# S5 set-up in a fused mixer layer: its parameters are transposed eight places of the weight stream behind their fetch instead of one

## The chip, the cores and the metric

The kernel runs on one core of one Trainium2 chip. The metric is the device time of one execution in microseconds (us). The time before is the median of three runs, 1197.18 us (1196.2 to 1198.06). TensorE (PE) multiplies matrices, VectorE (DVE) does elementwise work and reductions, ScalarE (ACT) copies and activation functions, GpSimd (POOL) masks and some fetches, and SP issues most transfers.

## The reference

One decoder layer (D_MODEL 2048, 256 tokens, DEPTH 1) with three parallel token mixers:

```python
h = rms_norm(x, norm_w[i])
proj = h @ w_in[i]
(g_qkv, g_z, g_b, g_a, r_feat, r_z, s_u, s_z, gate_logits) = _split_cols(proj, SPLIT_SIZES)
o_a = gdn_branch(...)      # gated DeltaNet
o_b = rwkv7_branch(...)    # RWKV-7
o_c = s5_branch(s_u, s_z, s5_a_re[i], s5_a_im[i], s5_log_dt[i], ...)
branch_proj = jnp.einsum('blnc,ncd->blnd', branches, w_branch[i])
gates = jax.nn.sigmoid(gate_logits.reshape(bsz, seq, N_BRANCH, D_MODEL) + gate_b[i])
merged = jnp.sum(gates * branch_proj, axis=2)
x = x + (merged @ w_out[i])
return rms_norm(x, final_norm_w)
```

The S5 branch is a diagonal state-space model with 64 groups of 16 channels and 64 states a group. Its set-up turns three parameters, `a_re` and `a_im` (64 x 64 each) and `log_dt` (64), into the discrete coefficients that the scan needs:

```python
dt = jnp.exp(log_dt)[:, None]
mag = jnp.exp(a_re * dt)
ab_re, ab_im = mag * jnp.cos(a_im * dt), mag * jnp.sin(a_im * dt)
den = a_re * a_re + a_im * a_im
coef_re = ((ab_re - 1.0) * a_re + ab_im * a_im) / den
coef_im = (ab_im * a_re - (ab_re - 1.0) * a_im) / den
```

The products of the coefficients with `b` and `c`, a scan over the 256 tokens, a skip, a GELU and a GLU (`s5_glu_w`) follow.

## The kernel before

**The stream of weights.** Nearly all matmul work is one long stream of weight blocks. A block ("unit") is a tile of 128 x 1024 float32 values (512 KB). It is fetched on SP's queue (`load_unit`, L264) into one of four `raw` tiles, and split into a high and a low part, `whi` by ScalarE (L267) and `wlo` by VectorE (L268), three tiles each. Each of its eight k-steps is then multiplied three times: high by high, high by low, low by high (`mm_unit`, the matmuls recorded as L62). `run_stream` keeps two blocks loaded ahead in the order of the program.

**Mixer work between the blocks.** The small work of the three mixers is written as Python generators in named lanes. `pump` (L1103) is called behind the second, fourth and sixth of a block's eight k-steps and behind the block: four places a block, with two k-steps (six matmuls) from one place to the next. At each place each lane's `due` count falls by one, and while it is not above zero, the lane's generator is run to its next `yield`, whose number is added to the count. So the numbers in the yields space the steps of a lane in places. TensorE's instructions stay in the order of the program: every matmul and transpose goes through the object `pe`, which ties each to the one before. The other queues, SP's and VectorE's among them, are ordered by the framework's scheduler.

**The stretch of the change.** By about 612 us the input projections of all three mixers are done, the last of them S5's own input u (`got_su`, which stores u to memory as `uD`, L1092). The memory of the first stages (`fr`, with the tile pool `fp`) is released, and new tiles take its place. The lane `s` with `s5_all` is put up, and `run_stream(back1())` begins: for each of 16 column blocks, two gate projections (two units each; the first six of these gates are done earlier) and two branch projections (one unit each). `got_proj` takes the results into `merged`: L1250 for the first branch, L1252 and L1253 for the second. The first six units of this stream are therefore branch projections, the matmuls named `mm<-oT`. Behind `back1` come twelve units for S5's z path (`sz_job`). These two streams together have 384 places. Then `finish("s", "sm")` runs off whatever is left in S5's lanes, the results of S5 are split into `ysp`, and the second half of the stream begins: two z columns, the GLU's weights (which need `ysp`), the third branch and the output projection.

**The steps that the prediction follows.** `s5_setup` issues three small fetches on SP's queue (L1310, L1311, L1313: `a_re` and `a_im` into `s5raw`, `log_dt` into `s5ldt`). Then it yields. Its next step copies `log_dt`, spread over 64 columns, into the third part of `s5raw` on VectorE (L1315), transposes the three parts on TensorE (`s5t`), and copies them back as `s5par` (L1320). From there a long chain of small VectorE steps with a few on ScalarE works out the coefficients, spaced by further yields. When it ends, `s5_mats` (lane `sm`) and `s5_tile` (lane `s`) run over eight tiles of channels. For each tile, `s5_mats` fetches u back (`UX`, L1442) and `b` and `c`, builds `BX` on VectorE (L1457 to L1462) and transposes it on TensorE (`s5bt`). `s5_tile` ends with `s5y` on TensorE and the tile's part of the result `us` (L1602).

Of the kernel before, what the change touches and what calls it, by code (L numbers as in the profile page):

```python
# [36 lines left out]
def tile_trunk(  # L37
# [1270 lines left out]
    def s5_setup(sp):  # L1308
# [2 lines left out]
        nc.sync.dma_start(out=raw[:, 1], in_=s5_a_im[0].rearrange("(i g) n -> i (g n)", g=2))  # L1311
        ldt = sp.tile([32, 2], F32, name="s5ldt")
        nc.sync.dma_start(out=ldt, in_=s5_log_dt[0].rearrange("(i g) -> i g", g=2))  # L1313
        yield 1
        ve.tensor_copy(raw[:, 2].rearrange("p (g n) -> p g n", g=2), ldt.unsqueeze(2).to_broadcast([32, 2, 64]))  # L1315
        pt = br_bank("s5t")
        for j in range(3):
# [289 lines left out]
    def s5_all():  # L1607
        with tc.tile_pool(name="s5s", bufs=1, side="right") as sp:
            yield from s5_setup(sp)
        for t in range(8):  # L1610
            lane("sm", s5_mats(t))
        for t in range(8):
            yield from s5_tile(t)
# [146 lines left out]
```

## Time and profile before

| What | Value |
|---|---|
| median of three runs | 1197.18 us (1196.2 to 1198.06) |
| the profiled execution, whole | 1195.4 us |
| its span, first to last instruction | 1193.6 us |
| TensorE busy | 1168.8 us (98%) |
| VectorE busy | 905.6 us (76%) |
| ScalarE busy | 681.6 us (57%) |
| mean granted TensorE clock | 0.995 of full |
| moved by transfers | 203.97 MB, mean 171 GB/s |

The table is of one execution. Rows of the timeline give the start in us from the span's begin, the duration, the engine, the line of the kernel, the operation, the tile written and the tiles read; "x3" is a number of instructions merged into one row, and a bracket gives the idle time of the engine before it and what ended it. Line 62 and line 65 are helpers, through which all matmuls and all transposes go; there the tile names tell which step it is. Rows of the waits say who waited for whom, in us in total, the number of times, and the longest. The name of the one waited for is inferred from semaphore events, and a wait for several is put down to one of them. The ends of matmuls are modelled, so the distance from start to start tells more than a duration.

### The profile page before, as it was taken

How to read it: one execution, taken by the hardware profiler on the slowest of the kernel's cores; microseconds unless marked ns; L12 is line 12 of the kernel's file. 1: busy time of each engine (PE TensorE's matmuls, PEld its weight loads, DVE VectorE, ACT ScalarE, POOL GpSimd, SP SyncE). 2: the span in 40 equal slices, each digit the busy share in tenths (PEclk: the TensorE clock that was granted, in tenths of full speed). 3: DMA queues.
4: the chain of work that ended last, by engine and by line, in shares of the span. 5: the costliest groups of instructions: out<-in, count | busy, mean ns of one | idle time of the engine just before them, and what ended most of it. 6: DMA issues, size and time to landing. Idle time of an engine off the chain costs nothing. (4 is left out here: it accounts for less than half of the span.)

```text
span 1193.6 us, 29078 instructions
## 1 busy us (share of the span) xinstructions
PE 1168.8 (98%) x11534; PEld 1128.4 (95%) x11534; DVE 905.6 (76%) x2261; ACT 681.6 (57%) x1412; POOL 56.2 (5%) x92
## 2 busy tenths in 40 slices
PE   7999999999999999999989999999999999999997
PEld 7999999999999999999989999999999999999887
DVE  7879696879787888885569979999986665555555
ACT  5465767676767776766534555555544544444443
POOL 1000000000000000000020111111000000000000
PEclk9999999999999999999989999999999999999999
DMA  7766555555656555555657677777776666667763
GB/s 203 195 180 171 153 139 148 141 149 147 159 130 158 148 141 131 132 149 144 182 157 191 181 189 188 195 190 191 185 185 169 182 189 179 188 183 239 242 197 116
DMA packets 384642, 203.97 MB, mean 171 GB/s; under 512 B 38825, under 2 KB 376186, under 8 KB 384122
## 3 DMA queue, kind: packets, MB, share of 16 engines
q1 hardware_dynamic: 382650, 199.61, 62.1%
q0 software_dynamic: 1536, 1.58, 0.6%
q8 instruction: 91, 1.49, 0.5%
q10 hardware_dynamic: 320, 0.93, 0.2%
q14 instruction: 45, 0.37, 0.1%
HBM read 195.88 MB, written 6.18 MB: 169 GB/s over the span
## 5 line engine op out<-in xcount | busy, mean ns | idle before, releaser
L62 PE MATMUL mm<-hT,whi 128*128 128x256 f32 (+1 forms) x4160 | 782.1, 288 | 0.0
L62 PEld LDWEIGHTS mm<-hT,whi 128*128 128x128 f32 (+1 forms) x4160 | 644.6, 191 | 7.3 <-issue 1.2
L62 PE MATMUL mm<-hT,wlo 128*128 128x256 f32 (+1 forms) x2080 | 587.4, 282 | 0.0
L268 DVE TENSOR_TENSOR wlo<-raw,whi 128x1024 fp32r<-128x1024 f32 (+1 forms) x346 | 422.3, 1221 | 184.7 <-ACT whi L267 181.6
L267 ACT ACTIVATE whi<-raw 128x1024 fp32r<-128x1024 f32 (+1 forms) x346 | 365.2, 1056 | 320.2 <-PE mm L62 239.3
L62 PEld LDWEIGHTS mm<-hT,wlo 128*128 128x128 f32 (+1 forms) x2080 | 396.4, 191 | 0.0
L62 PE MATMUL mm<-oT,whi 128*128 128x256 f32 x768 | 142.8, 286 | 0.0
L62 PEld LDWEIGHTS mm<-oT,whi 128*128 128x128 f32 x768 | 120.9, 194 | 0.5 <-issue 0.4
L62 PE MATMUL mm<-oT,wlo 128*128 128x256 f32 x384 | 109.3, 285 | 0.0
L62 PE MATMUL mm<-whi,mT 128*128 128x512 f32 (+1 forms) x288 | 76.8, 354 | 0.0
L62 PEld LDWEIGHTS mm<-oT,wlo 128*128 128x128 f32 x384 | 74.2, 193 | 0.0
L62 PEld LDWEIGHTS mm<-whi,mT 128*128 128x128 f32 x288 | 51.2, 189 | 7.5
L62 PE MATMUL mm<-wlo,mT 128*128 128x512 f32 (+1 forms) x144 | 50.9, 354 | 0.0
L570 DVE TENSOR_TENSOR ivp<-ivZ,ivX 48x1 f32<-48x1 f32 (+14 forms) x120 | 34.6, 288 | 2.0
L688 DVE SCALAR_TENSOR_TENSOR scr<-mm,pv,scr 128x255 f32<-128x255 f32 (+2 forms) x72 | 34.1, 473 | 0.6
L62 PEld LDWEIGHTS mm<-wlo,mT 128*128 128x128 f32 x144 | 27.2, 189 | 3.8
L572 DVE TENSOR_REDUCE ivZ<-ivp 48x1 f32<-48x1 f32 (+14 forms) x120 | 27.3, 227 | 1.7
L62 PE MATMUL mm<-ysp,whi 128*128 128x256 f32 x128 | 23.1, 283 | 0.0
L1252 DVE SCALAR_TENSOR_TENSOR gate<-gate,mm 128x256 f32<-128x256 f32 x32 | 13.3, 417 | 12.1 <-PE mm L62 11.9
L1242 ACT ACTIVATE gate<-mm,hgate 128x256 f32<-128x256 f32 x48 | 22.1, 461 | 0.3
L691 ACT ACTIVATE gth<-scr 128x256 f32<-128x256 f32 x24 | 9.9, 414 | 21.4 <-DVE scr L688 17.8
L62 PEld LDWEIGHTS mm<-ysp,whi 128*128 128x128 f32 x128 | 19.8, 189 | 0.0
(541 smaller groups left out, 1278.4 us busy)
## 6 DMA issues: line engine op xcount, KB each, us to landing
raw<-in_w_in_dram SPq DMA_DIRECT2D x256, 512.0 KB
raw<-in_w_branch_dram SPq DMA_DIRECT2D x48, 512.0 KB
raw<-in_w_out_dram SPq DMA_DIRECT2D x32, 512.0 KB
raw<-in_s_glu_w_dram SPq DMA_DIRECT2D x8, 512.0 KB
xs<-in_x_dram SPq DMA_DIRECT2D x4, 512.0 KB
xr<-in_x_dram SPq DMA_DIRECT2D x2, 1024.0 KB
raw<-in_w_in_dram SPq DMA_DIRECT2D x4, 384.0 KB
gr<-grow SPq DMA_DIRECT2D x8, 128.0 KB
```

Of the source, the lines that this page charges most:

```text
L62: return self.put(nc.tensor.matmul(*a, **k).ins)
L267: u["top"] = lambda: se.activation(out=hi[:, 0:nn], in_=raw[:, 0:nn], func=AF.Copy)
L268: u["sub"] = lambda eng=ve: eng.tensor_tensor(out=lo[:, 0:nn], in0=raw[:, 0:nn], in1=hi[:, 0:nn].bitcast(F32), op=ALU.subtract)
L570: ve.tensor_tensor(out=pi, in0=Z[:, 0:i, 0:i].rearrange("p j c -> p c j"), in1=X[:, i, 0:i].unsqueeze(1).to_broadcast([8 * NU, i, i]), op= ...
L572: ve.tensor_reduce(out=Z[:, i, 0:i], in_=pi, axis=AX.X, op=ALU.add)
L688: ve.scalar_tensor_tensor(out=c[:, s:T], in0=p[:, 0:T - s], scalar=pv("cw", (3 - s) * 24 + col), in1=c[:, s:T], op0=ALU.mult, op1=ALU.add)
L691: se.activation(out=th, in_=c, func=AF.Tanh, scale=0.5)
L1242: se.activation(out=t, in_=pss[0][:, 0:T], func=AF.Tanh, scale=0.5, bias=hgate[:, b * 16 + i:b * 16 + i + 1])
L1252: ve.scalar_tensor_tensor(out=g, in0=g, scalar=1.0, in1=p0, op0=ALU.add, op1=ALU.mult)
```

## The change

One number: the first `yield` in `s5_setup`, between the issue of the three fetches and their first use, is 8 in place of 1. The numbers of all later yields stay as they are.

```diff
         nc.sync.dma_start(out=raw[:, 1], in_=s5_a_im[0].rearrange("(i g) n -> i (g n)", g=2))
         ldt = sp.tile([32, 2], F32, name="s5ldt")
         nc.sync.dma_start(out=ldt, in_=s5_log_dt[0].rearrange("(i g) -> i g", g=2))
-        yield 1
+        yield 8
         ve.tensor_copy(raw[:, 2].rearrange("p (g n) -> p g n", g=2), ldt.unsqueeze(2).to_broadcast([32, 2, 64]))
         pt = br_bank("s5t")
         for j in range(3):
```

## The prediction

> **What bounds the kernel now.** I read the page first, then who TensorE (PE) waits for, then the timelines of PE, of the transfer queue SP and of VectorE (DVE) around the place where PE waits.
>
> ```profile
> span 1193.6 us, 29078 instructions
> PE 1168.8 (98%) x11534; PEld 1128.4 (95%) x11534; DVE 905.6 (76%) x2261; ACT 681.6 (57%) x1412; POOL 56.2 (5%) x92
> ```
>
> PE is busy for 98% of the span. So a saving counts only where PE stands still or runs slowly. The list of what PE waited for, longest first, says where (us in total, times, longest):
>
> ```profile
> PE warm L65 <- DMA xs<-in_x_dram: 4.4, 1, 4.4
> PE s5t L65 <- DMA uD<-us: 4.0, 1, 4.0
> ```
>
> The first row is the start of the kernel. The second is the three transposes of S5's parameters, the step that the change moves. Asked from 600 us to the end, the same view gives this one row alone: after the s5t wait PE never waits again, so time saved there has a free way to the end. PE's timeline there (start, duration, engine, line, operation, count, idle before):
>
> ```profile
> 612.34 0.40 PE L62 MATMUL mm<-oT,whi 128*128 128x256 f32 x2
> ...
> 612.94 0.28 PE L62 MATMUL mm<-oT,wlo 128*128 128x256 f32 x1
> 617.21 0.69 PE L65 MATMUL s5t<-ident,s5raw 32*128 32x32 f32 x3 [3.99 <-DMA uD<-us]
> 617.82 0.80 PE L62 MATMUL mm<-oT,whi 128*128 128x256 f32 x2
> ...
> 622.47 0.55 PE L62 MATMUL mm<-oT,whi 128*128 128x256 f32 x2
> 622.85 0.28 PE L62 MATMUL mm<-oT,wlo 128*128 128x256 f32 x1
> 622.98 0.40 PE L62 MATMUL mm<-oT,whi 128*128 128x256 f32 x2
> ```
>
> Five matmuls lie between the starts 612.34 and 612.94, so one takes 0.12. After six of them PE could have gone on at 613.06; it stands until 617.21. Then eight groups of three (617.82 to 622.98, the first and the last shown) take 5.16 us where 24 x 0.12 = 2.88 would do. The stretches of time say why (stretch, length, busy time and count of PE, PEld, DVE, ACT, POOL; granted clock; DMA):
>
> ```profile
> 615.00:616.00 1.00, 0.00 (x0) 0.00 (x0) 0.85 (x1) 0.00 (x0) 1.00 (x2) 0.98 0.34 80
> 616.00:617.00 1.00, 0.00 (x0) 0.00 (x0) 0.00 (x0) 0.00 (x0) 1.00 (x2) 0.50 0.11 21
> ...
> 617.20:623.00 5.80, 5.79 (x28) 5.61 (x29) 3.57 (x19) 1.06 (x1) 4.49 (x10) 0.52 0.60 144
> 623.00:667.70 44.70, 44.70 (x374) 44.55 (x373) 43.00 (x172) 20.55 (x24) 0.25 (x1) 1.00 0.66 177
> ```
>
> The clock is granted in full until close to 616, falls to 0.50 some 2.8 us after PE stopped, is still 0.52 in the mean from 617.2 to 623, and is whole after that. The pause is paid twice, once in standing and once in slow matmuls.
>
> What PE waited for is named as a transfer; SP's queue and DVE show which:
>
> ```profile
> 613.68 0.34 SPq L1092 DMA_DIRECT2D uD<-us  x1
> 614.12 0.37 SPq L1310 DMA_DIRECT2D s5raw<-in_s_a_re_dram  x1
> 614.55 0.41 SPq L1311 DMA_DIRECT2D s5raw<-in_s_a_im_dram  x1
> 615.01 0.45 SPq L1313 DMA_DIRECT2D s5ldt<-in_s_log_dt_dram  x1
> ...
> 616.24 0.39 SPq L264 DMA_DIRECT2D raw<-in_w_in_dram  x1
> ```
>
> ```profile
> 614.63 1.23 DVE L268 TENSOR_TENSOR wlo<-raw,whi 128x1024 fp32r<-128x1024 f32 x1 [0.47 <-ACT whi L267]
> 617.31 0.22 DVE L1315 COPY s5raw<-s5ldt 32x128 f32<-32x128 f32 x1 [1.46 <-DMA s5ldt<-in_s_log_dt_dram]
> 617.93 0.26 DVE L1320 COPY s5par<-s5t 128x96 f32<-128x96 f32 x1 [0.40 <-PE s5t L65]
> ```
>
> The three fetches are issued between 614.12 and 615.46, behind the last uD store. The last one lets DVE's copy go at 617.31, 2.3 us after its issue began, and the third transpose needs that copy.
>
> **The change part by part.** One number moves. In pump (L1103) the lane's count falls by one at each place, and the lane is stepped on while its count is not above zero. At the first place the count is -1; with yield 1 it comes to 0 and the lane steps again at once, so fetch and transposes stand in the same place. With yield 8 it comes to 7: the transposes come seven places later. Two k-steps, six matmuls, lie between places, so 42 matmuls, 5.04 us at full clock, now stand between.
>
> What is removed. From 613.06 to 622.98 are 9.92 us for three transposes and 24 matmuls. Undisturbed, the matmuls take 2.88. For transposes at full clock the nearest row is the four of s5bt:
>
> ```profile
> 675.02 0.60 PE L65 MATMUL s5bt<-ident,BX 128*128 128x128 f32 x4
> 675.37 0.48 PE L62 MATMUL mm<-hT,whi 128*128 128x256 f32 x2
> ```
>
> 0.35 us from start to start, so three take 0.27. I take this, with 0 and the 0.61 of now (617.21 to 617.82) as ends. The gain is 9.92 - 2.88 - 0.27 = **6.77 us** (6.43 to 7.04; more is excluded, since PE waits for nothing else from 600 us on): 4.15 of standing, 2.28 of slow matmuls, 0.34 of slow transposes.
>
> [...]
>
> Where PE stands when the transposes now come. Place eight lies behind 48 matmuls of the stream, at 612.34 + 48 x 0.12 = 618.10. The fetches stay where they were in the program and wait for what they waited for, so DVE's copy can still go at 617.31 and end at 617.53, 0.57 us ahead of PE. That hides them; if the cover is gone, each us of lateness costs one.
>
> What is next late on PE at that point: the weights. The third weight block is split on DVE from 614.63 to 615.86 and is needed at 618.1 or after. The fourth can be taken when PE leaves the first, at 612.34 + 24 x 0.12 = 615.2, on ScalarE for
>
> ```profile
> 621.90 1.06 ACT L267 ACTIVATE whi<-raw 128x1024 fp32r<-128x1024 f32 x1 [7.31 <-issue]
> ```
>
> 1.06 us and then on DVE for 1.23: even if the copy goes first it is done at 617.53 + 1.23 = 618.8, and needed behind the third block at 618.4 + 2.88 = 621.3. None is late.
>
> What moves with it. Every later step of S5 keeps its distance in places and comes 7 places later. DVE loses something: while PE stood and ran slowly it did set-up work that must now share DVE with PE at full rate. The DVE time is in the rows of 617.20:623.00 and 623.00:667.70 above; of the weight splits (L268) alone the same view gives, from 617.2 to 667.7:
>
> ```profile
> 617.20:667.70 50.50, 18.32 (x15) 0.94 0.66 173
> ```
>
> The mixer's merges are L1250, five times in this stretch, and L1252 with L1253, four times each. One of either output (L1253 has the tile shape of L1252 and is taken at the same 0.42), and the end of S5's chain:
>
> ```profile
> 622.07 0.42 DVE L1250 SCALAR_TENSOR_TENSOR merged<-gate,mm 128x256 f32<-128x256 f32 x1 [1.35 <-PE mm L62]
> ...
> 625.34 0.42 DVE L1252 SCALAR_TENSOR_TENSOR gate<-gate,mm 128x256 f32<-128x256 f32 x1
> ...
> 667.21 0.42 DVE L1462 TENSOR_TENSOR BX<-s5t,s5t 128x256 f32<-128x256 f32 x1
> ```
>
> Thirteen of 0.42 are 5.46. Set-up work is 3.57 + 43.00 - 18.32 - 5.46 = 22.79 us. Of it 3.57 - 0.42 = 3.15 lies in the slow stretch, 19.64 in the 44.7 us at full rate: 0.44 us for each us. At that share the 3.15 cost 7.2 us. DVE starts the chain at 618.4 (after the transposes) instead of 617.93, so BX, the first result that PE needs, is done at 618.4 + 44.6 + 7.2 = 670.2. PE asks for it (s5bt, now 675.02) at 675.02 - 6.77 + 5.04 = 673.3. The margin shrinks from 7.4 us to about 3.1, but stays.
>
> At the other end, the last S5 tile must be split for the GLU (ysp) before PE multiplies it:
>
> ```profile
> L62 PE MATMUL mm<-ysp,whi x128: 279/282/321, 935.9 to 958.7; 128*128 128x256 f32 x128
> ...
> L105 DVE TENSOR_TENSOR ysp<-us,ysp x8: 417/418/419, 915.6 to 919.1; 128x256 fp32r<-128x256 f32 x8
> ```
>
> The last split ends at 919.5 (919.1 + 0.42), the first use is at 935.9: of 16.4 us of slack the 5.04 leave 11.4. By the yields, S5's lane now ends at place 366 of the 384 that this stretch of the stream has; seven more still fit.
>
> **The sum.** 6.77 us off the profiled execution, 1193.6 of span and 1.8 around it, 1195.4 in all: 1188.6. That execution is 1.78 under the median of the three runs (1196.2 to 1198.06), so for the median 1197.18 - 6.77 = **1190.4 us**.
>
> **The rivals.**
>
> *The wait comes back in DVE's queue.* In program order the copy of the step sizes (L1315) now stands behind the mixer's second output, that is behind L1252 and L1253 of that block. If DVE's queue keeps that order, the copy must wait for the second block's last matmul (ended near 618.3), then 0.42, 0.42 and its own 0.22: done near 619.4, and PE stands 1.1 us. With a weight split of 1.23 ahead of it too, 2.4. Both are shorter than the 2.8 us after which the clock fell, so nothing is added: 6.77 - 1.1 or 6.77 - 2.4, hence 1191.5 to 1192.8. For it: the order of the program. Against it: queues are ordered by when operands are due, and now the weight split at 614.63, which is emitted later than the copy, stands ahead of it. 13%.
>
> *The fetch itself is late, so that the change does not put work behind it.* If SP takes the three issues behind the weight block of 616.24, they go at 616.7 to 618.0 and, by the 2.3 us above, release DVE near 620.0: PE stands 1.9 us, 1192.3. If more of that queue comes first and they slip so far that PE stands as long as now (4.15), the clock falls again (2.6) and nothing is gained: 1197.2. Against it: the issues wait for the branch memory to come free and the uD store ahead of them, neither of which the change touches. 10%, half of it within the bound of no change.
>
> *Slower: BX comes late at s5bt.* DVE must do the 22.8 us at a share of 0.44 beside PE at full rate. The stretch is full already (43.0 of 44.7). If the order of the queues lets the share sink to 0.37, BX is done at 618.4 + 22.8 / 0.37 = 680.0. PE then stands 6.7 us at s5bt, the clock falls and costs another 2.6, and 9.3 - 6.77 = 2.5 us are lost: 1199.7. The point from which it decides: a wait of 6.77 - 2.6 = 4.2 us, BX at 677.5, a share of 0.39. For it: DVE's load. Against it: the weight splits have not fallen behind in that load, PE waiting for none of them. 7%, 1 of it within no change.
>
> **How the numbers follow.** My forecast, the whole gain, has 70%: 1190.4. Its own spread is that of the transposes (6.43 to 7.04) and of the runs, about 0.9 to either side: 1189.2 to 1191.7. The first rival brings 1192.8. So 1189.2 to 1192.8 holds these two cases, 83% less a little for the scatter of the runs; what is left out lies above it. About 0.2%, 2.4 us, is what a measurement can tell from no change. Faster by more: 70 + 13 + 5 = 88%. Within it: 5 + 1 = 6%. Slower: 6%.
>
> **What would show it.** Right: PE's list of waits has no s5t row, or one under 0.6 us; the granted clock is 1.00 in each microsecond from 612 to 626; the s5t transposes start near 618.1, between the second and third mixer block, 0.27 to 0.4 us long; DVE's copy ends before them, near 617.5; s5bt starts near 673.3 with BX done near 670; the span is 1186.8. Wrong in the first step: an s5t wait of 1 to 2.5 us with DVE as its releaser and the merges ahead of the copy. Wrong in the second: the s5raw issues of SP behind 616.24. Wrong in sign: a new s5bt wait of over 4 us with the clock at 0.50 behind it. The sum itself is wrong if the s5t wait is gone, no other has come, and the span has not fallen by 6.4 to 7.1 us.

## The result and the profile after

The changed kernel takes 1189.8 us (median of six runs, 1188.95 to 1191.17), the kernel before 1196.24 (six runs, 1195.15 to 1198.06). The ratio is 0.9946, with a 95% interval of 0.9933 to 0.9959: 6.4 us or 0.54% faster. The prediction was 1190.4, counted from 1197.18, the median of the three runs it had; the six runs lie 0.94 lower. The profiled execution took 1189.7 us, with a span of 1188.0 in place of 1193.6.

The two longest rows of what PE waited for, over the whole span of the kernel after:

```profile
PE warm L65 <- DMA xs<-in_x_dram: 4.1, 1, 4.1
PE nwp L65 <- DMA sc<-in_norm_w_dram: 3.9, 1, 3.9
```

There is no s5t row any more, here or further down. PE's timeline at the place, after (start, duration, engine, line, operation, count):

```profile
613.44 0.40 PE L62 MATMUL mm<-oT,whi 128*128 128x256 f32 x2
...
619.08 0.28 PE L62 MATMUL mm<-oT,wlo 128*128 128x256 f32 x1
619.29 0.37 PE L65 MATMUL s5t<-ident,s5raw 32*128 32x32 f32 x3
619.59 0.51 PE L62 MATMUL mm<-oT,whi 128*128 128x256 f32 x2
...
622.57 0.40 PE L62 MATMUL mm<-oT,whi 128*128 128x256 f32 x2
```

From 613.44 to 619.20 (619.08 + 0.12) lie 48 matmuls at 0.12 us: two whole blocks. The transposes follow 0.09 later, and 0.39 after 619.20 the next block begins; that block's 24 matmuls take 2.98 (619.59 to 622.57). The clock, in the stretches around it (the granted clock is the third number from the end):

```profile
612.00:616.00 4.00, 4.00 (x36) 4.00 (x35) 2.41 (x8) 1.69 (x4) 0.87 (x2) 1.00 0.80 232
616.00:620.00 4.00, 4.00 (x35) 3.83 (x34) 3.24 (x7) 1.73 (x2) 3.96 (x8) 1.00 0.57 138
620.00:626.00 6.00, 6.00 (x52) 6.00 (x52) 5.51 (x20) 1.92 (x3) 2.73 (x5) 1.00 0.96 240
```

It stays whole, where it was at 0.50 before. The fetches on SP, after:

```profile
614.78 0.34 SPq L1092 DMA_DIRECT2D uD<-us  x1
615.22 0.37 SPq L1310 DMA_DIRECT2D s5raw<-in_s_a_re_dram  x1
615.64 0.41 SPq L1311 DMA_DIRECT2D s5raw<-in_s_a_im_dram  x1
616.11 0.44 SPq L1313 DMA_DIRECT2D s5ldt<-in_s_log_dt_dram  x1
...
617.23 0.39 SPq L264 DMA_DIRECT2D raw<-in_w_in_dram  x1
```

They stand in the same order behind the same store. The store and the three fetches are 1.1 us later on the span's clock, as is the first branch matmul (612.34 before, 613.44 after); the weight block behind them is 0.99 later (616.24 before). The programs are the same up to there. The difference comes from about 100 us earlier. In the kernel after, the clock falls for a while at 511, after a wait that stands in both profiles (the two stretches of after):

```profile
511.00:513.00 2.00, 1.92 (x10) 1.92 (x11) 1.51 (x3) 1.90 (x9) 0.00 (x0) 0.59 0.45 118
513.00:515.00 2.00, 2.00 (x12) 1.66 (x11) 1.03 (x3) 1.68 (x5) 0.00 (x0) 0.56 1.00 248
```

The last section comes back to this. To leave the time ahead of the change out, I compare a **stretch**: from the first branch matmul to the first matmul of the GLU. Its end, after:

```profile
930.57 0.40 PE L62 MATMUL mm<-ysp,whi 128*128 128x256 f32 x2
```

Before it was 935.93 - 612.34 = 323.59 us (the same row there starts at 935.93), after it is 930.57 - 613.44 = 317.13. So 6.46 us are gained in the stretch, and the span's 5.6 is smaller because the 1.10 lost earlier stands against it. By the prediction's own sign, a span that falls by less than 6.4 would mean a wrong sum; the missing part lies ahead of the change, and the stretch itself falls by 6.46.

### The profile page after: what moved, and what is told of

It is laid out like the page before. It is cut to its first block, busy times and chain, and to the rows that moved or that the text cites. A ratio compares the mean times of both kernels' runs of the same rounds, so it can differ in the third digit from the quotient of the medians.

```text
span 1188.0 us, 29064 instructions
## 1 busy us (share of the span) xinstructions
PE 1167.2 (98%) x11534; PEld 1127.5 (95%) x11534; DVE 905.0 (76%) x2261; ACT 680.5 (57%) x1412; POOL 56.0 (5%) x92
## 4 chain that ended last, share of the span: by engine, by line
PE 94%; DVE 2%; DMA 1%; ACT 1%; issue 0%; SPq 0%; DVEq 0%; ACTq 0%
PE mm L62 83%; PE s5y L62 1%; DVE wlo L268 1%; PE rg L62 1%; PE g L62 1%; PE gg L62 1%; DMA xs<-in_x_dram 1%; PE rw L62 1%; PE ryo L62 1%; PE warm L65 0%; DMA ivT<-zD 0%; PE s5u L62 0%; PE re L62 0%; PE rv L62 0%; PE rd L62 0%; PE ivy L62 0%
## 5 line engine op out<-in xcount | busy, mean ns | idle before, releaser
L1242 ACT ACTIVATE gate<-mm,hgate 128x256 f32<-128x256 f32 x48 | 22.1, 461 | 0.3
L1252 DVE SCALAR_TENSOR_TENSOR gate<-gate,mm 128x256 f32<-128x256 f32 x32 | 13.3, 417 | 11.4 <-PE mm L62 11.3
```

What stands on the lines that cost most here:

```text
L1242: se.activation(out=t, in_=pss[0][:, 0:T], func=AF.Tanh, scale=0.5, bias=hgate[:, b * 16 + i:b * 16 + i + 1])
L1252: ve.scalar_tensor_tensor(out=g, in0=g, scalar=1.0, in1=p0, op0=ALU.add, op1=ALU.mult)
```

## The experiments

My theory: PE stood for the latency of the fetch, and then ran at half clock because it had stood; work put between removes both. Rival 1: the gain comes from S5's later steps falling on other places of the stream. Rival 2: the half clock has nothing to do with this pause. Every stretch below is taken from one profile by the two rows named above, so it is one execution's. "Before" in a ratio is the kernel before on the same chip; the runs were made on different chips (the kernel before has a median of 1195.93 us on one, 1194.58 on another), so the ratios can be compared with one another, and the times only within one chip.

**The fetch early, the places as before.** The three fetches leave `s5_setup` and are issued ahead of S5's input projection; one transpose of 96 rows takes the place of three (parts of the edit are left out, marked by dots).

```diff
+    s5raw = cp.tile([96, P], F32, name="s5raw")
+    nc.sync.dma_start(out=s5raw[0:32], in_=s5_a_re[0]...)
+    nc.sync.dma_start(out=s5raw[32:64], in_=s5_a_im[0]...)
+    s5ldt = cp.tile([96, 2], F32, name="s5ldt")
+    nc.sync.dma_start(out=s5ldt[64:96], in_=s5_log_dt[0]...)
     run_stream(front_su())
...
         yield 1
...
-        for j in range(3):
-            pe.transpose(pt[:, j * 32:(j + 1) * 32], raw[:, j], ident[:32, :32])
+        pe.transpose(pt[:, 0:96], s5raw, ident[:96, :96])
```

> The yield stays 1; the three fetches go into a tile of their own before S5's input projection, and one transpose of 96 rows takes the place of three of 32. My theory (PE stands for the fetch and then runs at half clock): the wait is gone without any later step being moved; no s5t wait, clock 1.00 from 612 to 626, about 6.7 us less than before, 1189.5. Rival 1 (the gain comes from S5's steps falling on other places of the stream): the places are those of before, so no gain, 1196.2.

Measured: 1190.78 us, ratio 0.9959 (0.9945 to 0.9973). PE's timeline:

```profile
613.33 0.40 PE L62 MATMUL mm<-oT,whi 128*128 128x256 f32 x2
...
614.05 0.25 PE L65 MATMUL s5t<-ident,s5raw 96*128 96x96 f32 x1
614.08 0.48 PE L62 MATMUL mm<-oT,whi 128*128 128x256 f32 x2
...
930.96 0.40 PE L62 MATMUL mm<-ysp,whi 128*128 128x256 f32 x2
```

The transpose stands at the old place, six matmuls into the first block, and does not wait. The stretch is 930.96 - 613.33 = 317.63, 5.96 less than before. Rival 1 foresaw no gain here, so it falls as the cause of the main gain. The gain is less than the 6.7 that I expected, and the stretch is 0.5 us longer than the changed kernel's, although the one transpose takes 0.03 of PE's time (614.05 to 614.08) and the three there 0.39. So about 0.9 us are lost later; 0.3 of that is a wait that neither kernel has, and where the rest went is not shown:

```profile
PE mm L62 <- ACT gate L1242: 0.3, 1, 0.3
```

So in this profile it does matter where S5's steps fall, for less than a microsecond. The medians cannot show it: the intervals of the two ratios overlap.

**Dummy work in the pause.**

```diff
         yield 1
+        warm(ident, 40)
```

> The yield stays 1; 40 dummy transposes of the identity, about 0.10 us each, stand ahead of the three s5t transposes, so that PE works while it waits. My theory: the standing (4.1 us) is only filled, the clock stays at 1.00, and the clock's share of the sum alone is gained: 2.6 us less than before, 1193.6 (0.4 more or less with the length of the dummies). Rival 2 (the half clock does not come from this pause): the clock still falls near 616 and nothing is gained, 1196.2.

Measured: 1193.54 us, ratio 0.9979 (0.997 to 0.9988).

```profile
614.36 0.40 PE L62 MATMUL mm<-oT,whi 128*128 128x256 f32 x2
...
615.08 4.53 PE L65 MATMUL warm<-ident 128*128 128x128 f32 x40
619.54 0.43 PE L65 MATMUL s5t<-ident,s5raw 32*128 32x32 f32 x3
...
935.84 0.40 PE L62 MATMUL mm<-ysp,whi 128*128 128x256 f32 x2
```

The dummies take 4.46 us (615.08 to 619.54), 0.31 more than PE stood before. The clock at and behind them:

```profile
616.00:620.00 4.00, 4.00 (x38) 3.79 (x35) 1.61 (x5) 0.60 (x1) 3.96 (x6) 1.00 0.57 149
620.00:624.00 4.00, 4.00 (x34) 4.00 (x35) 3.62 (x18) 1.06 (x1) 3.60 (x8) 1.00 0.69 177
```

The clock stays whole in both. The stretch from branch to GLU is 321.48, a gain of 2.11; the clock's 2.6 (2.28 + 0.34) less the 0.31 of the longer dummies is 2.3. So the half clock comes from the pause (rival 2 falls), and the two terms of the sum are told apart: the clock's share by this run, the standing by the rest.

**Fewer places: yields 5, 3, 6 and 7.** The edit is the one number in each.

```diff
-        yield 1
+        yield 5      # then 3, 6, 7 in kernels of their own
```

> Yield 5, four places in place of seven: PE comes to the transposes at 613.06 + 4 x 0.72 = 615.94 by the clock of the profile before, 1.3 us ahead of the release at 617.2. My theory: an s5t wait of 1.3 us, too short for the clock to fall, so 6.65 - 1.3 = 5.4 us less than before, 1190.8. Rival 1: no order in the number of places. Rival 2: the clock falls all the same, 1193.4.

> Yield 3, two places: PE comes to the transposes at 613.06 + 1.44 = 614.50 by the clock of the profile before, 2.7 us ahead of the release. My theory: 1.44 us are gained by the work put between; the clock falls in most runs, as it did with yield 5, for one or two stretches of 3.41 us (0 to 1.3 us less clock loss than now). From the first branch matmul to the first GLU matmul 321 to 322.2 us (now 323.6), the time 1193.5 to 1194.8. A pause shorter than 2.8 us that leaves the clock alone, as my prediction had it, would give 319.6 and 1192.2.

> Yield 6, five places: PE comes at 616.66, 0.6 us ahead of the release. My theory: an s5t wait of 0.5 to 0.9 us; the clock falls in few runs. From the first branch matmul to the first GLU matmul 317.8 us, the time 1190.4. If any pause here costs the clock for 3.41 us, 319.3 and 1191.9.

> Yield 7, six places: PE comes at 617.38, just behind the release of the fetch. My theory: the fetch is hidden; a wait of 0 to 0.5 us is left if DVE's copy stands behind the fourth weight split. From the first branch matmul to the first GLU matmul 317.1 to 317.6 us, the time 1189.8.

| yield | places between | s5t wait, us | stretch, us | clock below full there | time, us (ratio to before) |
|---|---|---|---|---|---|
| 1 | 0 | 3.99 | 323.59 | 6.8 us | before |
| 3 | 2 | 2.57 + 0.20 | 321.64 | 3.4 us | 1193.5 (0.9988; 0.9979 to 0.9998) |
| 5 | 4 | 1.14 + 0.32 | 320.26 | 3.4 us | 1192.14 (0.9961; 0.9946 to 0.9977) |
| 6 | 5 | 0.31 + 0.43 | 318.13 | none | 1189.54 (0.9958; 0.9943 to 0.9973) |
| 7 | 6 | none listed | 317.59 | none | 1189.04 (0.9957; 0.994 to 0.9973) |
| 8 | 7 | none | 317.13 | none | 1189.8 (0.9946; 0.9933 to 0.9959) |

The waits fall by 0.6 to 0.7 us a place until the fetch is hidden, near the 0.72 that a place takes and as my theory has it. With yield 7 no wait is listed, but the three transposes take 0.62 where they take 0.37 after: PE has their slot at 616.30, and the third is still held for DVE's copy, which is done at 616.71. The stretches with yields 3 and 7 lie in the ranges expected, the one with yield 6 is 0.3 over the 317.8 expected. The expectation for yield 5 failed in one point. PE's timeline there, and the stretches of 3.41 us around it:

```profile
617.11 0.28 PE L62 MATMUL mm<-oT,wlo 128*128 128x256 f32 x1
618.54 0.28 PE L65 MATMUL s5t<-ident,s5raw 32*128 32x32 f32 x2 [1.14 <-DMA uD<-us]
619.14 0.24 PE L65 MATMUL s5t<-ident,s5raw 32*128 32x32 f32 x1 [0.32 <-DVE s5raw L1315]
619.31 0.50 PE L62 MATMUL mm<-oT,whi 128*128 128x256 f32 x2
```

```profile
616.97:620.38 3.41, 1.94 (x16) 1.62 (x15) 2.72 (x8) 0.73 (x1) 3.37 (x7) 1.00 0.57 148
620.38:623.79 3.41, 3.41 (x19) 3.41 (x18) 2.48 (x15) 1.06 (x1) 2.56 (x5) 0.50 0.99 244
623.79:627.20 3.41, 3.41 (x30) 3.41 (x30) 3.07 (x17) 1.06 (x1) 0.00 (x0) 1.00 0.30 81
```

The pause was 1.5 us in all and PE had been at work again for a microsecond, and still the clock fell, for one stretch of 3.41 us. The five runs of this kernel lie in two groups, 1192.14 to 1193.36 with a mean granted clock of 0.996 to 0.997, and 1189.25 and 1189.26 with 0.998. It may be that the same short pause costs the clock in some executions and not in others, but this is not shown: the mean takes in the whole span, and the profiled executions with yields 6 and 7 have 0.997 with no fall at this place (with yield 7, for one, it is 1.00 in every 3.41 us from 23.04 to 1180.16). With yield 3 the clock fell too, so its second expectation (a pause that leaves the clock alone) did not come.

**More places: yields 16 and 26.**

> Yield 16, 15 places. My theory: with seven places the wait is gone already, and S5's lane still ends at place 381 of 384, so the time is that of the changed kernel, 1189.8 within 0.5. Rival 1: another time, since every step of S5 falls elsewhere. If the shrinking slack at the end of S5 costs something, a wait at s5y or ysp.

> Yield 26, 25 places: S5's lane would end at place 391 of 384, so the end of its last tile is run off with no stream between. My theory: no s5t wait, the clock full there, but PE now waits at the last s5y for the DVE steps ahead of it, 2 to 3.5 us. From the first branch matmul to the first GLU matmul 319 to 320.6 us, the time 1192 to 1193.5. If the end of S5 has more slack than its places, 317.1 and 1189.8.

Yield 16: 1189.43 us, ratio 0.9944 (0.9929 to 0.9959); stretch 928.92 - 611.89 = 317.03. No wait comes in place of the one removed and nothing more is gained: from seven places to fifteen the number does not matter. Rival 1 would have it matter.

Yield 26: 1190.76 us, ratio 0.9967 (0.9956 to 0.9979); stretch 930.82 - 611.41 = 319.41. The stretch is in the range that I expected; the time is below it (1192 to 1193.5), though that range was counted from the times of the main result (1196.24 before), and before was 1194.58 on the chip of this run. The cause is another than I expected. PE does not wait at s5y at all. Its waits from 560 us on are these:

```profile
PE mm L62 <- ACT gate L1242: 1.9, 2, 1.4
```

ScalarE, in the longest of them:

```profile
667.59 1.06 ACT L267 ACTIVATE whi<-raw 128x1024 fp32r<-128x1024 f32 x1 [2.01 <-PE mm L62]
673.24 0.26 ACT L1531 ACTIVATE s5cc<-cb 128x64 f32<-128x64 f32 x1 [4.59 <-DVE cb L1406]
673.40 1.04 ACT L267 ACTIVATE whi<-raw 128x1024 fp32r<-128x1024 f32 x1
674.35 0.46 ACT L1242 ACTIVATE gate<-mm,hgate 128x256 f32<-128x256 f32 x1
```

ScalarE's queue stands 4.59 us at a copy of S5's first tile (L1531) for its input `cb` from DVE. The weight split and the gate behind it are late, and PE waits for the gate, 1.43 us. The other wait, 0.43, has another reason:

```profile
653.87 1.28 ACT L1242 ACT_TABLE_LOAD   x1
655.16 0.47 ACT L1242 ACTIVATE gate<-mm,hgate 128x256 f32<-128x256 f32 x1
```

```profile
655.69 0.51 PE L62 MATMUL mm<-hT,whi 128*128 128x256 f32 x2 [0.43 <-ACT gate L1242]
```

S5's sine (L1367) and a weight split ran on ScalarE ahead of this gate, and then the gate's line, L1242, loads a table for 1.28 us before the gate itself. From 640 us to 680 ScalarE loads tables four times here (at 651.19, 653.87, 655.66 and 662.71), and twice in the kernels before (643.93, 652.21) and after (643.88, 646.87), each time for 1.28 us. The wait with yield 7 is of the same kind (load at 645.13, gate at 646.42, PE 0.2 us late). The last s5y had slack: its last input on DVE was done at 913.64, and PE came to it at 917.74. So my reason for this run fell, and a smaller form of rival 1 stands: when S5 is moved, one of its steps can come to stand ahead of the gate in ScalarE's queue. By the lists of waits that cost 0.2 us with yield 7, 0.3 with the early fetch, 1.9 here, and nothing with yields 8 and 16.

## Why the prediction was right, by its steps

**The pause is the cost, and it is paid twice.** Right. The sum was 6.77 us, 4.15 of standing, 2.28 and 0.34 of slow work. The stretch gained 6.46. The 0.31 between them can be placed. The s5t transposes at full clock took 0.39 from the slot they could have had (619.20 to 619.59), where the prediction took 0.27 from s5bt: 0.12. The 24 matmuls behind them take 2.98, not 2.88: 0.10. And at 648.69 PE starts a block 0.20 late, behind a gate that is done at 648.63; before, the same block (654.04) is 0.11 late: 0.09. That the time itself came within 0.6 of the forecast is in part chance: the median before, from six runs, is 0.94 below the base of the forecast, and the gain is 0.33 below its sum (6.44 for 6.77). The dummies, which keep the clock but not the time, gained 2.11 of the 2.6.

**The fetch is hidden when PE comes.** Right, with less to spare, and for another reason. DVE's queue, after:

```profile
617.54 1.22 DVE L268 TENSOR_TENSOR wlo<-raw,whi 128x1024 fp32r<-128x1024 f32 x1 [0.26 <-ACT whi L267]
618.68 0.21 DVE L1315 COPY s5raw<-s5ldt 32x128 f32<-32x128 f32 x1
619.39 0.42 DVE L1252 SCALAR_TENSOR_TENSOR gate<-gate,mm 128x256 f32<-128x256 f32 x1 [0.51 <-PE mm L62]
619.73 0.25 DVE L1320 COPY s5par<-s5t 128x96 f32<-128x96 f32 x1
```

The copy is done at 618.89, which is 617.79 on the clock of before, in place of 617.53: it is held no longer by the fetch but by the fourth weight split. It is 0.31 us ahead of PE's free slot, not 0.57. With yield 6 this shows as a wait of 0.43 for L1315. The first rival had the copy behind L1252 and L1253; it stands ahead of both. As in the kernel before, a weight split that comes later in the program stands ahead of the copy.

**The first rival's price** held a wrong rule: that a pause shorter than the 2.8 us after which the clock fell adds nothing. With yield 5 a pause of 1.14 + 0.32 did cost the clock. With yield 3 the waits of 2.57 + 0.20 cost 4.51 against yield 8 (321.64 - 317.13), so 1.7 beyond their length. Had the rival come, 1192.8 could have been too low an upper end. The half clock lasts 3.41 us with yields 3 and 5, and twice that, about 6.8, in the kernel before (a mean of 0.98 in 615 to 616 sets its begin at 615.96, one of 0.61 in 622 to 623 its end at 622.78).

**The rest of S5 comes later, at no cost.** Right in sign, mis-sized at s5bt. The rows after:

```profile
666.81 0.41 DVE L1462 TENSOR_TENSOR BX<-s5t,s5t 128x256 f32<-128x256 f32 x1
```

```profile
674.71 0.60 PE L65 MATMUL s5bt<-ident,BX 128*128 128x128 f32 x4
```

On the clock of before s5bt comes at 673.6 (673.3 was predicted), but BX is done at 666.1 and not 670.2: the margin is 7.5 us, as large as before, not 3.1. The step that failed is the share of DVE, taken as fixed at 0.44 us of set-up for each us. Over the set-up (619.60 to 667.20) DVE was busy

```profile
619.60:623.00 3.40, 3.40 (x29) 3.40 (x29) 3.09 (x11) 1.14 (x2) 3.09 (x7) 1.00 1.10 283
623.00:667.20 44.20, 44.16 (x368) 43.95 (x367) 43.13 (x178) 21.56 (x26) 0.15 (x1) 1.00 0.73 193
```

for 46.22 of 47.60 us; before, for 46.57 of 50.50. DVE's idle time fell from 3.9 us to 1.4: much of what it had done under PE's pause it now does in time in which it had waited. At the end of S5 the slack is 13.5 us (the last ysp split ends at 917.0, by a last start of 916.6, the first use is at 930.57), where 11.4 was predicted.

**The fetch late on SP, and the loss at s5bt.** Neither came: the issues are in the same order, and no wait at s5bt appears with any number of places.

## What to carry to other kernels

A wait of TensorE, where it bounds the kernel, can cost more than its length in the list of waits, since the clock may fall behind it: for 3.41 us with yields 3 and 5, for twice that in the kernel before. Here 4 us of waiting cost 6.5. The fetch was hidden once the independent work put between was about as long as the 4.15 us that PE had stood: five places (3.6 us) left waits of 0.74, six (4.3) none in the list. The effect was whole with seven places, fifteen gave nothing more, and twenty-five lost 2.3 us of the stretch. Before a chain is moved, look at what its steps will stand ahead of in the other engines' queues, not only at when its results are due.

## What the runs showed of the hardware that was not expected

The clock does not follow a pause by its length alone: one of 1.5 us cost it with yield 5, and the two waits of 0.9 and 0.3 us near 510 us cost it in one profile of ten. In all ten profiles PE waits 0.9 and then 0.3 us there (the rq transposes, for ryn from ScalarE), and only in the profile of the changed kernel does the clock fall behind them. In two profiles these rows begin within 0.34 us of each other, before and after:

```profile
510.83 0.33 PE L65 MATMUL rq<-ident,ryn 128*128 128x128 f32 x1 [0.90 <-ACT ryn L1069]
```

```profile
510.49 0.33 PE L65 MATMUL rq<-ident,ryn 128*128 128x128 f32 x1 [0.90 <-ACT ryn L1069]
```

By the first branch matmul the second is 1.10 us behind, so the fall cost about 1.4. Where the pause lies against the times at which the clock changes does not explain this either. In the two kernels' profiles these times lie whole multiples of 3.413 us apart: before, the clock falls at 615.96, is whole again at 622.78 and falls at 1189.40, 2 and 168 multiples behind the first; after, it falls at 511.36, is whole at 514.77 and falls at 1183.78, 1 and 197 multiples behind. Counted back in slices of this length from the fall behind the s5t wait, 619.07 with yield 3 and 620.38 with yield 5, 32 slices lead in both to one that holds both rq waits, as one does in the kernel after. The first row here is the changed kernel's, whose clock falls at its end; the second is yield 3's and the third yield 5's, whose clock does not fall there; the fourth is a slice with less PE work, 134 ahead of yield 3's fall, which passed without a fall (PE busy is the first number behind the length):

```profile
507.95:511.36 3.41, 2.25 (x39) 1.00 0.96 262
509.85:513.26 3.41, 2.23 (x18) 1.00 0.65 178
511.15:514.56 3.41, 2.24 (x17) 1.00 0.66 174
161.69:165.10 3.41, 2.02 (x16) 1.00 0.45 133
```

Ahead of the fall behind s5t, PE was busy 1.94 of 3.41 us with yield 5, and 1.30 with yield 3. So no single amount of PE work in a slice, as the profile shows it, parts the falls from the rest, and what decides stays open.

Up to the first branch matmul the ten profiles scatter from 611.26 to 614.36 us, though nearly all of them run the same program to there. From the first GLU matmul to the end they scatter by 0.8 only (257.4 to 258.1). So in these profiles most of the scatter outside the stretch lies ahead of it, which is the reason for comparing a stretch. The fall near 511 is not its cause: the profiles at the two ends, yield 7 (611.26) and the dummies (614.36), have the clock at 1.00 there.
